# Zero-padded and regrouped small matmuls in a two-block network on one core

## The chip, the core and the metric

The kernel runs on one core of a Trainium2 chip. The metric is the device time of one execution in microseconds, the median of three runs. Five engines work side by side, each through its own queue in program order: TensorE (PE, the matmuls, with its weight loads shown apart as PEld), VectorE (DVE), ScalarE (ACT), GpSimd (POOL) and SyncE (SP, which here issues most of the DMAs).

## The reference

Two networks run one after the other on a sequence of 512 tokens of width 1024, all in float32. The first has two layers. Layer 0 mixes tokens by windowed averages and by an attention of 8 heads (96 query channels, 64 value channels); layer 1 by a neighbourhood attention of 16 heads of 64 channels. Each layer then attends to 256 memory tokens and has an MLP. The second network has two layers of retention (4 heads) and gated linear attention (GLA, 4 heads, keys of 64 channels, values of 128), run forwards and backwards over 512 latent and 256 context tokens, and an MLP. What the change touches is this:

```python
# layer 0 of the first network: attention
p = softmax(s); o = einsum('bhqk,bkhd->bqhd', p, v)          # d = 64
# layer 1: neighbourhood attention
s = einsum('bchd,brckhd->bhcrk', q_row, k_win) * scale + bias # d = 64
# second network: GLA gate, with 16 + 16 gate channels
a = log_sigmoid(d @ up + ub) / 16
# GLA in chunks of 64 tokens, forwards and backwards: within a chunk
#   o += mask(q k^T) v, between chunks o += q S, S <- decay * S + k^T v
```

## The kernel before, in words

Large products are written as three float32r matmuls of high and low halves (`mat3`: hi·hi, hi·lo, lo·hi), from 128x128 weights against 256 or 512 columns. `linear` and `linear_tm` stream the weights for them through SP, ACT (`whi`, L247) and DVE (`wlo`, L248). Attention and GLA use plain float32 matmuls (`mat`, L159) and PE transposes (`tr`, L171). A float32 matmul stands in the trace as two passes (two MATMUL records), a float32r matmul or a transpose as one.

Work is written as Python generators ("streams") that a small planner, `run`, interleaves by an estimated TensorE clock; a `yield 1500` lets other streams go first for about that many ns. A scheduler then fixes each engine's order when the program is built, by its own estimate of times. The result is one fixed order for each engine, in which long runs of float32r matmuls of the projections are mixed with the small matmuls of attention and GLA.

The small matmuls do not use the whole 128x128 array of TensorE. The built program gives each a tile of the array (rows x columns):

- `values` in `mixer0` (L785 to 809): softmax rows are transposed (four `tr` into an `mm` buffer), copied to `PT` by ACT or DVE, and multiplied with the values, 64 output rows of 512 columns: tile 128x64. Heads `hh` 0 and 1 go to different halves of the array's columns. For each of 4 key blocks `j` and 4 pairs of heads there are two such matmuls, 32 in all.
- `unit` in `mixer1` (L940 to 992): scores `pt<-kT,qT` contract over 64 channels: tile 64x128. One tile `qT` holds two heads, one in each half of the rows. There are 64 such matmuls, 32 of 256 and 32 of 192 columns. The products with the values (`po<-PT,v` and `po<-PT,vs`, 128 columns) have tiles 128x64 or 64x64.
- `gla` in `hybrid`: the gate `pt<-dd,gup` contracts over 32 channels (tile 32x128; 8 of 512 columns and 8 of 256). The masked products `pt<-gc,ei` and the state updates `pt<-v,ke` contract over 64 rows (tile 64x128), for two directions or two chunks in different halves of the rows; the forward ones are all written before the backward ones. In the output the products with the states (`po<-S,gc`, tile 128x64, two halves of columns) stand as pairs behind a full matmul `po<-v,gp`:

```python
for i in range(n):
    self.mat(po[:, sl(i)], pr[:, sl(i)], V["g", hd, i], True, False)
    for j in range(2):
        cix = 2 * i + j
        self.mat(po[64 * j:64 * j + 64, sl(i)], c[:, sl(cix, 64)], S[cix], False, True)
```

GLA runs 4 context heads (n = 2 blocks of 128 tokens) and 4 latent heads (n = 4) in layer 0, 4 latent heads with outputs and 4 context heads that only carry the state in layer 1. The matmuls `bank<-ada,sil` (four column quarters of 32, tile 128x32) and `gate_in` (L1263) are of this kind too and stay as they are.

## Time and profile before

| | before |
|---|---|
| median of 3 runs | 3273.99 us (3270.78 to 3279.21) |
| the profiled execution | 3278.94 us |
| its span, first to last instruction | 3277.2 us |
| PE busy | 3195.6 us, 98% |
| PEld busy | 2669.8 us, 81% |
| DVE busy | 1787.2 us, 55% |
| ACT busy | 1204.8 us, 37% |
| POOL busy | 206.9 us, 6% |
| mean granted clock of TensorE | 0.985 of full speed |

Full speed of TensorE's clock is 2.4 GHz, the other level 1.2 GHz. A row of the timeline merges equal instructions that follow each other: its start, the time from the first one's start to the last one's end, and how many passes. A matmul's end is modelled and overlaps the next one's start, so the price of a piece of work is the distance between starts.

### The profile page before, as it was taken

How to read it: one execution, taken by the hardware profiler on the slowest of the kernel's cores; microseconds unless marked ns; L12 is line 12 of the kernel's file. 1: busy time of each engine (PE TensorE's matmuls, PEld its weight loads, DVE VectorE, ACT ScalarE, POOL GpSimd, SP SyncE). 2: the span in 40 equal slices, each digit the busy share in tenths (PEclk: the TensorE clock that was granted, in tenths of full speed). 3: DMA queues.
4: the chain of work that ended last, by engine and by line, in shares of the span. 5: the costliest groups of instructions: out<-in, count | busy, mean ns of one | idle time of the engine just before them, and what ended most of it. 6: DMA issues, size and time to landing. Idle time of an engine off the chain costs nothing.

```text
span 3277.2 us, 45112 instructions
## 1 busy us (share of the span) xinstructions
PE 3195.6 (98%) x17942; PEld 2669.8 (81%) x17942; DVE 1787.2 (55%) x3208; ACT 1204.8 (37%) x2157; POOL 206.9 (6%) x257
## 2 busy tenths in 40 slices
PE   8999999999999999999999999999999989899998
PEld 8856678888987878888988987888888879778887
DVE  6863364445556564445775786333334756774444
ACT  5733242223444432223553534121222534342223
POOL 0100000000112000000021312000000012200000
PEclk9999999999999999999999999999999999899999
DMA  5357743333321223333533221222212423123332
GB/s 155 116 165 240 255 148 99 98 98 102 89 71 53 85 78 97 98 98 91 153 90 88 84 84 58 65 65 65 64 60 60 131 78 97 39 74 98 99 97 71
DMA packets 301858, 323.99 MB, mean 99 GB/s; under 512 B 18832, under 2 KB 270608, under 8 KB 301648
## 3 DMA queue, kind: packets, MB, share of 16 engines
q1 hardware_dynamic: 296656, 315.22, 31.2%
q10 hardware_dynamic: 4992, 5.90, 0.6%
q8 instruction: 141, 2.31, 0.3%
q14 instruction: 69, 0.57, 0.1%
HBM read 310.05 MB, written 2.10 MB: 95 GB/s over the span
## 4 chain that ended last, share of the span: by engine, by line
PE 93%; DVE 3%; ACT 1%; DMA 1%; issue 1%; SPq 0%; ACTq 0%; DVEq 0%
PE mm L159 79%; PE pt L159 6%; PE po L159 4%; PE bank L1032 2%; PE pt L171 1%; PE bank L159 1%; DMA raw<-in_w_mem_kv 1%; PE mm L171 0%; DVE wlo L248 0%; DVE S L1455 0%; DVE sq L366 0%; ACT whi L247 0%; DVE o L1300 0%; DVE ht L1068 0%; DMA ada<-in_ada_w 0%
## 5 line engine op out<-in xcount | busy, mean ns | idle before, releaser
L248 DVE TENSOR_TENSOR wlo<-raw,whi 128x1024 fp32r<-128x1024 f32 (+2 forms) x503 | 595.9, 1186 | 720.3 <-ACT whi L247 690.6
L247 ACT CAST whi<-raw 128x1024 fp32r<-128x1024 f32 (+2 forms) x503 | 505.0, 1006 | 1234.2 <-PE mm L159 1077.5
L159 PE MATMUL mm<-hi,whi 128*128 128x512 f32 (+2 forms) x2768 | 886.5, 357 | 15.3 <-DVE cx L1135 6.1
L159 PE MATMUL mm<-hi,wlo 128*128 128x512 f32 (+2 forms) x2288 | 842.2, 369 | 0.0
L159 PE MATMUL mm<-lo,whi 128*128 128x512 f32 (+2 forms) x1808 | 706.2, 391 | 1.7 <-DVE lo L1073 1.6
L159 PEld LDWEIGHTS mm<-hi,whi 128*128 128x128 f32 (+1 forms) x2768 | 493.8, 190 | 104.5 <-issue 15.2
L159 PEld LDWEIGHTS mm<-hi,wlo 128*128 128x128 f32 (+1 forms) x2288 | 433.4, 190 | 79.7 <-issue 10.0
L159 PE MATMUL mm<-ahi,whi 128*128 128x512 f32 (+1 forms) x1552 | 489.7, 352 | 0.0
L159 PE MATMUL mm<-ahi,wlo 128*128 128x512 f32 (+1 forms) x1296 | 471.8, 366 | 0.0
L159 PEld LDWEIGHTS mm<-lo,whi 128*128 128x128 f32 (+1 forms) x1808 | 340.7, 188 | 77.9 <-issue 7.4
L159 PE MATMUL mm<-alo,whi 128*128 128x512 f32 (+1 forms) x1040 | 399.6, 386 | 0.0
L159 PE MATMUL mm<-whi,hi 128*128 128x256 f32 (+2 forms) x1392 | 368.3, 292 | 17.5 <-ACT v L1207 7.6
L159 PE MATMUL mm<-wlo,hi 128*128 128x256 f32 (+2 forms) x1200 | 346.2, 289 | 2.2 <-DVE wlo L248 2.2
L159 PEld LDWEIGHTS mm<-ahi,whi 128*128 128x128 f32 x1552 | 277.4, 189 | 41.0
L159 PE MATMUL mm<-whi,lo 128*128 128x256 f32 (+2 forms) x1008 | 289.4, 289 | 0.6 <-DVE lo L406 0.6
L159 PEld LDWEIGHTS mm<-whi,hi 128*128 128x128 f32 x1392 | 258.4, 195 | 26.7 <-ACT v L1207 7.8
L159 PEld LDWEIGHTS mm<-ahi,wlo 128*128 128x128 f32 x1296 | 244.4, 189 | 39.4
L159 PEld LDWEIGHTS mm<-wlo,hi 128*128 128x128 f32 x1200 | 234.3, 195 | 9.4 <-issue 5.3
L159 PEld LDWEIGHTS mm<-alo,whi 128*128 128x128 f32 x1040 | 195.5, 188 | 38.1
L159 PEld LDWEIGHTS mm<-whi,lo 128*128 128x128 f32 x1008 | 195.9, 195 | 5.6 <-issue 4.8
L1135 DVE SCALAR_TENSOR_TENSOR x<-mm,mod,x 128x512 f32<-128x512 f32 (+1 forms) x102 | 72.2, 717 | 99.5 <-PE mm L159 99.1
L952 POOL TENSOR_TENSOR bm<-bias,mask 128x192 f32<-128x192 f32 (+1 forms) x64 | 45.5, 735 | 839.5 <-DMA mask<-in_na_mask 643.6
(320 smaller groups left out, 3249.9 us busy)
## 6 DMA issues: line engine op xcount, KB each, us to landing
raw<-in_w_ff SPq DMA_DIRECT2D x128, 512.0 KB, 3.6
raw<-in_w_mlp SPq DMA_DIRECT2D x128, 512.0 KB, 3.6
raw<-in_w_in SPq DMA_DIRECT2D x98, 512.0 KB, 3.8
ada<-in_ada_w SPq DMA_DIRECT2D x192, 256.0 KB, 4.5
raw<-in_w_qkv SPq DMA_DIRECT2D x24, 512.0 KB, 3.7
raw<-in_w_out SPq DMA_DIRECT2D x24, 512.0 KB, 3.4
raw<-in_w_mem_kv SPq DMA_DIRECT2D x32, 256.0 KB, 3.7
raw<-in_w_mem_q SPq DMA_DIRECT2D x16, 512.0 KB, 3.5
```

The lines of the kernel that those rows point to most:

```text
L159: return self.nc.tensor.matmul(out, lhsT=lhsT, rhs=rhs, start=start, stop=stop, **k).ins
L171: self.nc.tensor.transpose(out, in_, self.ident)
L247: nc.scalar.copy(hi[:, v], raw[:, v])
L248: nc.vector.tensor_sub(lo[:, v], raw[:, v], f32(hi[:, v]))
L952: nc.gpsimd.tensor_add(bm[:, sl(hh, 256)][:, :n], o.tab[hp * 2 + hh][:, f0:f0 + n], masks[(0, 1, 1, 2)[b]][:, f0:f0 + n])
L1032: m = nc.tensor.matmul(p[32 * g:32 * g + 32], lhsT=sil[:, k], rhs=w, start=(k == 0), stop=(k == KT - 1), tile_position=(0, 32 * g)).ins
L1135: self.nc.vector.scalar_tensor_tensor(x, p, self.mod[l][:, 16 + 24 * j + m, st:st + 1], x, ALU.mult, ALU.add)
```

## The change

The products of `values` wait until two key blocks are copied and then stand as four matmuls together, the first of them made to wait for the two last copies. The scores of `unit` read a `qT` of 128 rows in which the other head's half is zero (its gain `gg` is zero there), so that each has the full tile 128x128; two ACT copies make two such tiles where one made one. `gup` and `dd` get 128 rows, of which 96 are zero (set by POOL). The two halves of `pt<-gc,ei` and of `pt<-v,ke` are written in turns, and the products with the states stand behind all full matmuls of their output.

```diff
 def values(pr):                                        # mixer0
-            last = None
-            for j in range(5):
-                ts = []
-                for hh in range(2 if j < 4 else 0):
+            ts = []
+            for j in range(4):
+                for hh in range(2):
                     ...
                     t = self.t2(nm="PT")
-                    (nc.vector.tensor_copy if j % 2 else nc.scalar.copy)(t, p)
-                    ts.append(t)
+                    copied = (nc.vector.tensor_copy if hh else nc.scalar.copy)(t, p).ins
+                    ts.append((j, hh, t, copied))
                     self.give("mm")
-                if last:
-                    yield 500
-                    for hh in range(2):
-                        self.mat(po[sl(hh, 64)], vt[pr, j - 1][:, sl(hh, 64)], last[hh], j == 1, j == 4)
-                last = ts
+                if j % 2:
+                    yield 1500
+                    first = None
+                    for j, hh, t, _ in ts:
+                        m = self.mat(po[sl(hh, 64)], vt[pr, j][:, sl(hh, 64)], t, j == 0, j == 3)
+                        first = first or m
+                    self.wait_for(first, ts[-2][3], ts[-1][3])
+                    ts = []
                 yield 0
@@ mixer1
-        ng, gg = self.tiny(2, "ng"), self.tiny(1, "gg")
+        ng, gg = self.tiny(2, "ng"), self.tiny(2, "gg")
         nc.scalar.dma_start(ng, A["na_g"])
-        nc.vector.tensor_scalar(gg, ng[:, 0:1], ng[:, 1:2], 0.125, ALU.mult, ALU.mult)
+        nc.gpsimd.memset(gg, 0.0)
+        for hh in range(2):
+            f = sl(hh, 64)
+            nc.vector.tensor_scalar(gg[f, hh:hh + 1], ng[f, 0:1], ng[f, 1:2], 0.125, ALU.mult, ALU.mult)
...
-                        nc.scalar.activation(t, p, AF.Copy, scale=gg)
-                        o.q.append(t)
+                        o.q.append([self.t2(nm="qT") for _ in range(2)])
+                        for hh, t in enumerate(o.q[-1]):
+                            nc.scalar.activation(t, p, AF.Copy, scale=gg[:, hh:hh + 1])
...
-                rows = slice(64 * hh, 64 * hh + 64)
                 p = self.pt((128, n))
-                self.mat(p, o.q[hp][rows, sl(b)], o.k[hp][rows, k0:k1])
+                self.mat(p, o.q[hp][hh][:, sl(b)], o.k[hp][:, k0:k1])
@@ second network
-        self.gup = self.cst("gup", [32, 4, 128])
+        self.gup = self.cst("gup", [128, 4, 128])
+        nc.gpsimd.memset(self.gup, 0.0)
...
-        nc.scalar.dma_start(self.gup, self.A["gup"][:, l])
+        nc.scalar.dma_start(self.gup[:32], self.A["gup"][:, l])
...
             t = self.t2(nm="dd", w=w)
+            nc.gpsimd.memset(t, 0.0)
             nc.scalar.copy(t[:32], p)
...
-            self.mat(p, self.gup[:, hd], F["d"][:32])
+            self.mat(p, self.gup[:, hd], F["d"])
...
-                for d, s in enumerate((f, r)):
-                    p = self.pt((128, w))
-                    for i in range(n):
+                ps = [self.pt((128, w)) for _ in range(2)]
+                for i in range(n):
+                    for p, s in zip(ps, (f, r)):
                         self.mat(p[:, sl(i)], ei[s, sl(i)], c[s, sl(i)])
+                for d, p in enumerate(ps):
                     nc.vector.copy_predicated(pr, self.gmask[:, d, :w], p)
...
-            for q in range(2):
-                rs = sl(q, 64)
-                p = self.pt((128, n, 128))
-                for i in range(n):
-                    self.mat(p[:, i], ke[rs, sl(i)], V["g", hd, i][rs])
-                    ups[2 * i + q] = p[:, i]
+            ps = [self.pt((128, n, 128)) for _ in range(2)]
+            for i in range(n):
+                for q in range(2):
+                    rs = sl(q, 64)
+                    self.mat(ps[q][:, i], ke[rs, sl(i)], V["g", hd, i][rs])
+                    ups[2 * i + q] = ps[q][:, i]
...
+            k = {"skip_group_check": True}
             for i in range(n):
-                self.mat(po[:, sl(i)], pr[:, sl(i)], V["g", hd, i], True, False)
-                for j in range(2):
-                    cix = 2 * i + j
-                    self.mat(po[64 * j:64 * j + 64, sl(i)], c[:, sl(cix, 64)], S[cix], False, True)
+                self.mat(po[:, sl(i)], pr[:, sl(i)], V["g", hd, i], i == 0, False, **k)
+            for cix in range(nch):
+                i, j = divmod(cix, 2)
+                self.mat(po[64 * j:64 * j + 64, sl(i)], c[:, sl(cix, 64)], S[cix], False, cix == nch - 1, **k)
```

The order of the instructions on PE moves in three places. The rows name the output buffer, the operands and the shape of the output; x2 stands for two equal rows. First, PE in `values` of the first pair of heads, before:

```order
L171 MATMUL mm_2267<-ident,P_1961 128x128
L159 MATMUL po_2245<-PT_2251,v_1511 64x512
L159 MATMUL pt_2330<-hi_1997,hi_1988 128x512
L159 MATMUL pt_2330<-lo_1998,hi_1988 128x512
L159 MATMUL pt_2330<-hi_1997,lo_1989 128x512
L159 MATMUL po_2245<-PT_2258,v_1511 64x512
```

and in the change:

```order
L159 MATMUL pt_2384<-hi_1997,hi_1988 128x512
L159 MATMUL pt_2384<-lo_1998,hi_1988 128x512
L159 MATMUL pt_2384<-hi_1997,lo_1989 128x512
L159 MATMUL po_2245<-PT_2251,v_1511 64x512
L159 MATMUL po_2245<-PT_2258,v_1511 64x512
L159 MATMUL po_2245<-PT_2265,v_1511 64x512
L159 MATMUL po_2245<-PT_2272,v_1511 64x512
L171 MATMUL mm_2328<-ident,P_1877 128x128
```

The four products of two key blocks, which stood apart between scores and transposes, now stand together. Second, PE at the output of GLA head 0 of the latent tokens in layer 0, before:

```order
L159 MATMUL po_15792<-S_15714,gc_15088 64x128 x2
L159 MATMUL po_15792<-v_15248,gp_15566 128x128
L159 MATMUL po_15792<-S_15714,gc_15088 64x128 x2
L159 MATMUL po_15792<-v_15250,gp_15566 128x128
L159 MATMUL po_15792<-S_15715,gc_15088 64x128 x2
L159 MATMUL po_15792<-v_15250,gp_15566 128x128
L159 MATMUL po_15792<-S_15715,gc_15088 64x128 x2
```

and in the change:

```order
L159 MATMUL pt_15754<-v_15269,ke_15711 128x128 x2
L159 MATMUL pt_15754<-v_15271,ke_15711 128x128 x2
L159 MATMUL po_15813<-S_15735,gc_15109 64x128 x4
L159 MATMUL po_15813<-S_15736,gc_15109 64x128 x4
L159 MATMUL mm_15919<-whi_15922,lo_13619 128x256
```

The eight products with the states are one group; the full matmuls `po<-v,gp` have gone ahead of it. Third, PE at the state updates of a latent GLA head of layer 0 (`ke_16897`), before:

```order
L159 MATMUL pt_16930<-v_15412,ke_16897 128x128 x2
L159 MATMUL pt_16930<-v_15414,ke_16897 128x128 x2
L159 MATMUL pt_16935<-v_15412,ke_16897 128x128 x2
L159 MATMUL pt_16935<-v_15414,ke_16897 128x128 x2
L159 MATMUL mm_16987<-wlo_17108,hi_13622 128x256
```

and in the change (the same head is `ke_16918`):

```order
L159 MATMUL pt_16951<-v_15433,ke_16918 128x128 x2
L159 MATMUL pt_16951<-v_15435,ke_16918 128x128 x2
L159 MATMUL po_17063<-v_15433,gp_16756 128x128
L159 MATMUL po_17063<-v_15435,gp_16756 128x128 x2
L159 MATMUL mm_17008<-whi_17128,hi_13636 128x256
L159 MATMUL mm_17008<-wlo_17129,hi_13636 128x256
L159 MATMUL mm_17008<-whi_17128,lo_13637 128x256
L159 MATMUL mm_17008<-whi_17128,hi_13642 128x256
L159 MATMUL mm_17008<-wlo_17129,hi_13642 128x256
L159 MATMUL mm_17008<-whi_17128,lo_13643 128x256
L159 MATMUL mm_17008<-whi_17128,hi_13648 128x256
L159 MATMUL pt_16952<-v_15433,ke_16918 128x128 x2
```

Written in turns, the two halves have come to stand apart in the built order: the second half (`pt_16952`) is behind three full matmuls of the output and seven float32r matmuls.

## Rows read from the trace of the kernel before

**Rows 1.** The page, parts 1 and 4: busy times, and the chain by engine.

```profile
PE 3195.6 (98%) x17942; PEld 2669.8 (81%) x17942; DVE 1787.2 (55%) x3208; ACT 1204.8 (37%) x2157; POOL 206.9 (6%) x257
...
PE 93%; DVE 3%; ACT 1%; DMA 1%; issue 1%; SPq 0%; ACTq 0%; DVEq 0%
```

**Rows 2.** Busy time by stage: us, then busy PE, PEld, DVE, ACT, POOL; clock, DMA share, GB/s.

```profile
150.00:310.00 160.00, 158.72 (x789) 94.00 (x788) 89.06 (x197) 60.40 (x117) 0.31 (x1) 0.99 0.60 195
840.00:1070.00 230.00, 225.11 (x1551) 183.92 (x1550) 138.59 (x393) 103.52 (x260) 41.55 (x58) 0.97 0.22 68
1550.00:1900.00 350.00, 340.03 (x2402) 304.37 (x2400) 244.40 (x441) 164.49 (x291) 59.56 (x62) 0.98 0.36 102
2520.00:2850.00 330.00, 306.37 (x2001) 267.58 (x2000) 216.10 (x392) 141.57 (x246) 44.27 (x46) 0.93 0.30 86
```

**Rows 3.** Timeline of PE, two value products together: start us, us, instruction (rows x columns).

```profile
176.16 0.39 PE L159 MATMUL mm<-lo,whi 128*128 128x512 f32 x1
176.38 0.39 PE L159 MATMUL mm<-hi,wlo 128*128 128x512 f32 x1
176.70 1.08 PE L159 MATMUL po<-PT,v 128*64 128x512 f32 x4
177.71 0.50 PE L159 MATMUL pt<-hi,hi 96*128 96x512 f32 x1
```

**Rows 4.** Timeline of PE, one value product alone.

```profile
158.40 1.07 PE L159 MATMUL po<-PT,v 128*64 128x512 f32 x2
```

**Rows 5.** Timeline of PE: sixteen passes of the modulation, four to each column quarter.

```profile
254.74 1.92 PE L1032 MATMUL bank<-ada,sil 128*32 128x512 f32 x16
```

**Rows 6.** Timeline of PE, scores: alone (256, 192 columns) and a pair (192).

```profile
852.49 0.28 PE L159 MATMUL mm<-wlo,hi 128*128 128x256 f32 x1
852.70 0.70 PE L159 MATMUL pt<-kT,qT 64*128 64x256 f32 x2
853.32 0.39 PE L159 MATMUL mm<-whi,lo 128*128 128x256 f32 x1
...
873.47 0.59 PE L159 MATMUL pt<-kT,qT 64*128 64x192 f32 x2
...
1039.61 0.59 PE L159 MATMUL pt<-kT,qT 64*128 64x192 f32 x4
```

**Rows 7.** Timeline of PE, full-array float32 matmuls of the memory attention.

```profile
358.75 1.03 PE L159 MATMUL pt<-mk,q 128*128 128x256 f32 x4
359.61 1.88 PE L159 MATMUL po<-PT,mv 128*128 128x512 f32 x4
361.33 1.03 PE L159 MATMUL pt<-mk,q 128*128 128x256 f32 x4
```

**Rows 8.** Timeline of PE, the gate's matmul: 256 and 512 columns.

```profile
1645.09 0.69 PE L159 MATMUL pt<-dd,gup 32*128 32x256 f32 x2
...
1694.33 1.12 PE L159 MATMUL pt<-dd,gup 32*128 32x512 f32 x2
```

**Rows 9.** Timeline of PE: two pairs (neighbourhood values) and one pair (GLA states).

```profile
909.41 0.66 PE L159 MATMUL po<-PT,vs 128*64 128x128 f32 x8
...
1606.25 0.44 PE L159 MATMUL po<-S,gc 128*64 128x128 f32 x4
```

**Rows 10.** Timeline of PE: halves of four and four passes, one of eight, two of eight.

```profile
1592.69 0.72 PE L159 MATMUL pt<-gc,ei 64*128 64x128 f32 x8
...
1739.89 1.16 PE L159 MATMUL pt<-gc,ei 64*128 64x128 f32 x8
...
1880.89 1.71 PE L159 MATMUL pt<-v,ke 64*128 64x128 f32 x16
```

**Rows 11.** Groups by line: copies to PT and to qT (busy us, mean ns, idle before).

```profile
L798 DVE COPY PT<-mm 128x512 f32<-128x512 f32 x16 | 11.0, 686 | 10.0 <-PE mm L171 8.8 <-PE po L159 1.2
...
L933 ACT ACTIVATE qT<-pt,gg 128x512 f32<-128x512 f32 x8 | 5.3, 685 | 4.7 <-PE mm L159 2.6 <-PE pt L171 2.2
```

**Rows 12.** Longest wait of PE from 2520 to 2850 us: total, times, longest.

```profile
PE mm L159 <- ACT v L1207: 7.6, 1, 7.6
```

More of the change, by code (lines that the diff above doesn't have):

```diff
@@ L930, in transposes @@
                         self.tr(p[:, sl(i)], o.tm[nm, i // 2][:, sl(i % 2, 256)][:, sl(j)])
-                    t = self.t2(nm=nm + "T")
                     if nm == "q":
-                        nc.scalar.activation(t, p, AF.Copy, scale=gg)
-                        o.q.append(t)
+                        o.q.append([self.t2(nm="qT") for _ in range(2)])
+                        for hh, t in enumerate(o.q[-1]):
+                            nc.scalar.activation(t, p, AF.Copy, scale=gg[:, hh:hh + 1])
                     else:
+                        t = self.t2(nm="kT")
                         nc.vector.tensor_copy(t, p)
```

## The prediction

> **What bounds the kernel now.** TensorE does. On the page PE is busy for 98% of the span and 93% of the chain that ended last is PE [rows 1]; DVE has 55% and ACT 37%. In the stages that the change touches (150 to 310 us: attention of layer 0; 840 to 1070: neighbourhood attention; 1550 to 1900 and 2520 to 2850: the GLA layers) PE stands idle for 1.3, 4.9, 10.0 and 23.6 us, while DVE has at most 244 of 350 us of work [rows 2]. So what counts is how much time of PE's queue each small matmul takes. The order of instructions on PE is fixed when the kernel is built; outside these stages the two programs hardly differ.
>
> The next view is the timeline of PE, read by starts. A float32r matmul of 512 columns starts 0.22 us after the one before (176.16, 176.38). The value products on half of the columns start 0.32 after it, at 176.70: about 0.09 us more. They hold PE until 177.71 [rows 3]. Around the score it is the same: the float32r matmul of 256 columns, elsewhere 0.12 us, is followed after 0.21 us, and the next one starts 0.62 us after the score [rows 6]. So a stretch on a part of the array costs about 0.09 us at its entry, some more inside and at its exit. Its **price**, the distance from the start before it to the start behind it less the step that the matmul before needs anyway, is 177.71 - 176.38 - 0.23 = 1.10 us in rows 3 and 853.32 - 852.49 - 0.12 = 0.71 in rows 6. Both are the row's own length plus 0.02 (1.08, 0.70), and I use that sum for the other stretches.
>
> Full-array float32 passes have no such step: four of 256 columns take 359.61 - 358.75 = 0.86, that is 0.43 for a matmul of two passes; four of 512 take 1.72, 0.86 for a matmul [rows 7].
>
> **The change, part by part.** How often each kind of stretch stands in PE's queue I counted in the two fixed orders.
>
> Value products of layer 0. Of 32 matmuls 8 pairs stand together and 16 matmuls alone: 24 stretches. A pair costs 1.10 [rows 3], one alone 1.09 [rows 4]: a pair on two halves of the columns runs side by side, and the lone one pays for both. Three of the lone ones touch a stretch of the modulation and share its step, so 26.1 us in all. Now there are 8 stretches of four. Sixteen passes, four to each column quarter, cost 1.94 [rows 5]; eight passes on two halves are also four to each part, so I take 1.94 and get 15.5. If a second pair cost as much as a first (2.20) it would be 17.6. Term: -10.6, bound -8.5. The new wait for both last copies stands behind 2 us or more of other PE work in all 8 places, and a copy takes 0.69 us [rows 11]; that cover hides it, and if DVE were late the transposes behind it would wait too.
>
> Scores. 28 of 64 stand alone, 22 of 256 and 6 of 192 columns: 22 x 0.72 + 6 x 0.61 = 19.5 [rows 6]. With all rows they cost 0.43 for 256 [rows 7]; a full float32 pass of 192 columns is in no row, it lies between 0.22 (128 columns, half of 0.43) and 0.43, and by columns at 0.33: 22 x 0.43 + 6 x 0.33 = 11.4. That is -8.1. The other 36 stand in pairs or beside value products. A pair of 192 costs 0.61 now (0.59 + 0.02, [rows 6]) and 0.66 padded, so each of 18 pairs loses 0.05, 0.9 in all. Term: -7.2; bounds -4 (192 columns as dear as 256, and another 2 us of steps at the value products that now stand alone) and -9. On ACT come 8 copies of 0.69 us [rows 11], 5.5 us beside 103.5 of 230 [rows 2]; TensorE waits for them only at a group's start.
>
> The row of the pair speaks against padding, and so does a rule of the Trainium skill (TensorEngine Tiling (Array Packing), When to Use Tiling): with a contraction of 64 or less, tile the rows two ways, for up to twice the speed. By it the scores would stay in halves and be brought together instead. By the rows, 32 pairs at the price of a pair would be at best level with 64 padded ones; padding wins because the built order parts 28 of them.
>
> Gate. 8 matmuls of 512 columns at 1.14 and 8 of 256 at 0.71 are 14.8, less 0.7 for four that touch another small stretch: 14.1 [rows 8]. Full: 8 x 0.86 + 8 x 0.43 = 10.3 [rows 7]. Term: -3.8. The memsets on POOL (12% busy there, [rows 2]) are short and early.
>
> States in the GLA output. 40 pairs at 0.46 are 18.4; two pairs cost 0.68, so a further pair 0.22 [rows 9]. Now 8 groups of four pairs (0.46 + 0.66 = 1.12) and 4 of two: 11.7. Term: -6.7.
>
> Masked products. Halves in sequence already overlap in part: four and four passes cost 0.74, one half of eight 1.18, and two of eight 1.73, not 2.36 [rows 10]. The context heads stand as before. Of 8 latent heads 4 stood together and 4 apart: 4 x 1.73 + 4 x 2.36 = 16.4. Now 3 stand in turns (0.74 + 2 x 0.22 = 1.18), one nearly so (1.4), 1 together, 3 apart: 13.8. Term: -2.6.
>
> That overlap is against a rule of the Trainium skill (TensorE: Matmul & The Clock Gate, Part 3, The mechanism): matmuls start and end strictly in program order. By it two halves of eight in sequence would cost 2.06 us (sixteen steps of 0.11 and the 0.30 that 1.18 has beyond eight), not 1.73, and the term would be some 1 us larger.
>
> State updates. Of 8 latent heads 3 stood together (1.73), none does now: the scheduler parts them, as the third order above shows. Term: 3 x 0.63 = +1.9. Written in turns and not standing in turns, this part does not do what it says.
>
> Sum: -10.6 - 7.2 - 3.8 - 6.7 - 2.6 + 1.9 = **-29.0 us** of PE's queue. Not all of it shortens the span: where PE waits for others (23.6 of 330 us in the last stage, [rows 2], the longest of them 7.6 us for ACT [rows 12]) a faster PE waits longer. I take 3 us back, about a quarter of what the GLA terms bring. The profiled execution took 3278.94 us (span 3277.2); less 26 it is 3252.9. The median of the runs is 4.95 us below the profiled one, so **3248 us**.
>
> **Rivals.** *Half of it turns into waits.* The GLA layers hold long chains between PE, DVE and ACT; all of their net 11.2 us and part of the scores' could come back as idle time. Against: the first stage and the scores have hardly any idle time [rows 2]. Time: 3274 - 29 + 13 = 3258.
>
> *Groups on halves do not overlap when they are long.* Then eight value passes cost 0.24 + 8 x 0.43 = 3.7 us (8 x 3.7 = 29.6, +3.5 instead of -10.6) and four state pairs 0.24 + 16 x 0.11 = 2.0, two 1.1 (8 x 2.0 + 4 x 1.1 = 20.4, +2.0 instead of -6.7): 3274 - 29 + 14 + 9 = 3268, no change that can be told. Against: the sixteen passes at 1.94 [rows 5].
>
> *Slower: the joint wait for the copies.* PE's queue is in order, so if at the 8 groups of value products the later copy is late, all float32r work behind it stands. It decides from 3.6 us a group on (29 / 8). At the length of the longest wait in rows 12, 7.6 us, it would be +61: 3274 - 29 + 61 = 3306. For: DVE and ACT also do the softmax of that stage. Against: DVE has 89 us of work in 160 [rows 2] and PE waits little there now.
>
> **How the numbers follow.** Forecast (3236 to 3256, the bounds of the terms and up to 8 us of waits) 0.74; half into waits 0.15; no overlap 0.06; slower 0.05. The likeliest gives 3248. Both ends outside the forecast are widened for small shifts of order elsewhere: 3233 to 3262. A measurement can tell about 0.3%, 10 us, so faster means below 3264: 0.74, 0.14 of the second and 0.01 of the third, 0.89; the same 0.07; slower 0.04.
>
> **What would show it.** The timeline should have `po<-PT,v x8` near 1.92 us, `po<-S,gc x16` near 1.10, scores as `128*128` rows with 0.22 us between their starts for 256 columns, and no steps around scores and gates. PE's busy time should fall by about 29 us, its idle time (81 us) rise by a few. The forecast is wrong if the x8 and x16 rows are much longer, if PE's idle time from 150 to 310 us grows by more than 5 us, or if the padded scores cost more than 0.43.

## The result and the profile after

| | before | after |
|---|---|---|
| median | 3272.39 us (3268.49 to 3279.21, 4 runs) | 3230.85 us (3229.87 to 3239.15, 4 runs) |
| after / before | | 0.9876, 95% interval 0.9853 to 0.9900 |
| profiled execution, its span | 3278.94 us, 3277.2 us | 3230.51 us, 3228.7 us |

The change takes 41.5 us off where 26 were forecast; 3230.85 lies 2 us below the lower end of the widened range (3233). The page of the changed kernel, parts 1 and 4, against [rows 1]:

```profile
PE 3146.0 (97%) x17942; PEld 2664.6 (83%) x17942; DVE 1779.2 (55%) x3209; ACT 1210.6 (37%) x2165; POOL 212.3 (7%) x263
...
PE 92%; DVE 5%; ACT 1%; DMA 1%; issue 1%; POOL 0%; DVEq 0%; SPq 0%; ACTq 0%; POOLq 0%
```

TensorE still sets the end. The profiled execution of before was a long one; a second profile of the same kernel (the run before_again, span 3269.6) lies nearer to the median, and the stages are compared with that. They are cut at the same instructions of every program: attention of layer 0; the stage of the scores, from the first score to the last memory attention of that layer; the first GLA layer; the stretch up to the next; the second GLA layer. The columns are those of [rows 2]. The kernel before, once more:

```profile
111.08:322.58 211.50, 208.42 (x1098) 134.83 (x1097) 130.78 (x332) 98.26 (x212) 6.37 (x16) 1.00 0.56 183
...
843.97:1154.91 310.94, 306.05 (x1924) 249.08 (x1924) 178.19 (x482) 142.22 (x341) 41.56 (x58) 0.98 0.23 70
...
1560.91:1906.85 345.94, 334.93 (x2368) 298.66 (x2367) 244.20 (x451) 160.94 (x287) 59.52 (x62) 0.98 0.34 100
1906.85:2542.04 635.19, 624.41 (x3625) 551.22 (x3623) 280.67 (x446) 192.10 (x328) 28.72 (x30) 1.00 0.21 66
2542.04:2828.04 286.00, 266.53 (x1797) 234.28 (x1797) 186.83 (x330) 117.34 (x198) 37.57 (x34) 0.95 0.31 90
```

and the changed kernel:

```profile
110.10:309.02 198.92, 194.59 (x1098) 134.31 (x1097) 130.30 (x333) 98.35 (x213) 6.84 (x18) 1.00 0.60 196
...
830.49:1129.12 298.63, 291.81 (x1924) 249.79 (x1923) 179.57 (x482) 145.94 (x347) 40.58 (x58) 1.00 0.24 73
...
1535.04:1866.23 331.19, 321.67 (x2348) 292.92 (x2346) 238.50 (x448) 160.96 (x287) 60.45 (x63) 0.99 0.36 102
1866.23:2505.02 638.79, 629.17 (x3647) 556.06 (x3644) 283.68 (x450) 192.57 (x329) 29.12 (x32) 0.99 0.22 67
2505.02:2786.79 281.77, 260.09 (x1798) 235.00 (x1797) 182.30 (x325) 117.39 (x198) 39.19 (x34) 0.94 0.33 92
```

The first two stages are 12.6 and 12.3 us shorter. The last three belong together (in the changed kernel 20 or so float32r matmuls stand behind the cut between them instead of ahead of it): 1267.1 us become 1251.8, 15.4 less. The other stages differ by 0.7 us in all. The terms of the forecast were 10.6, 7.2 and 11.2. Two things are to be seen beside that. Over all nine stages, which are nearly the whole run, PE's busy time fell by 43.5 us (3188.8 to 3145.3), while its idle time (length less busy) rose by 2.5 (67.1 to 69.6): by 1.3 in the first stage shown and 1.9 in the second, while in the last three it went from 41.3 to 40.8. And the clock column of the scores' stage went from 0.98 to 1.00: before has 10.2 us at half clock (0.50 of full speed) there by the clock records of its trace, the changed kernel none.

The new forms cost what was taken for them; the old ones had cost more. The timeline of PE in the changed kernel, a value group and scores, against [rows 3 to 7]:

```profile
161.18 1.94 PE L159 MATMUL po<-PT,v 128*64 128x512 f32 x8
...
834.57 0.28 PE L159 MATMUL mm<-wlo,hi 128*128 128x256 f32 x1
834.69 0.60 PE L159 MATMUL pt<-kT,qT 128*128 128x256 f32 x2
834.93 0.47 PE L159 MATMUL mm<-whi,lo 128*128 128x256 f32 x1
835.24 0.28 PE L159 MATMUL mm<-whi,hi 128*128 128x256 f32 x1
```

Eight passes of a value group last 1.94 (taken: 1.94). A padded score starts 0.12 after the matmul ahead of it, without the step of 0.09; from 834.57 to 835.24 are 0.67, less two float32r steps of 0.12 the score costs 0.43, the value taken. This span reaches to the second start behind the score. The price of a lone score before, 0.71, was read to the first start behind it. The kernel before goes on behind the score of [rows 6] with

```profile
853.55 0.28 PE L159 MATMUL mm<-whi,hi 128*128 128x256 f32 x1
853.66 0.29 PE L159 MATMUL mm<-wlo,hi 128*128 128x256 f32 x1
```

and behind the value products of [rows 3] with

```profile
178.05 0.39 PE L159 MATMUL pt<-lo,hi 96*128 96x512 f32 x1
```

The matmul behind the score, at 853.32, holds PE for 0.23 us until the next start, where such a matmul elsewhere holds it for 0.12; the one behind the value products, at 177.71, for 0.34 instead of 0.23. So a stretch on a part of the array has a step of 0.11 at its end too, and the step falls on the matmul behind it. Over the same span as in the change a lone score costs 853.55 - 852.49 - 2 x 0.12 = 0.82, and padding it brings 0.39 and not 0.28.

In the first GLA layer, against [rows 8 to 10]:

```profile
1576.58 0.66 PE L159 MATMUL po<-S,gc 128*64 128x128 f32 x8
...
1728.15 1.09 PE L159 MATMUL po<-S,gc 128*64 128x128 f32 x16
...
1819.33 1.02 PE L159 MATMUL pt<-dd,gup 128*128 128x512 f32 x2
...
1832.45 1.16 PE L159 MATMUL pt<-gc,ei 64*128 64x128 f32 x16
...
1844.51 1.16 PE L159 MATMUL pt<-v,ke 64*128 64x128 f32 x8
1846.75 1.16 PE L159 MATMUL pt<-v,ke 64*128 64x128 f32 x8
```

Four state pairs take 1.09 (taken: 1.12 with the steps), and a masked product in turns takes 1.16 for sixteen passes, as long as one half of eight alone. The two halves of a state update stand apart at 1.16 each, as the built order had shown. The full matmuls of the output, `po<-v,gp`, got cheaper with the state pairs. Between two pairs, before (the first pair is in [rows 9]), and together, in the change:

```profile
1606.62 0.49 PE L159 MATMUL po<-v,gp 128*128 128x128 f32 x2
1607.04 0.44 PE L159 MATMUL po<-S,gc 128*64 128x128 f32 x4
...
1732.27 1.06 PE L159 MATMUL po<-v,gp 128*128 128x128 f32 x8
1733.08 0.36 PE L159 MATMUL mm<-whi,hi 128*128 128x256 f32 x1
```

Between two pairs one of them holds PE for 0.42 us; four together hold it for 0.81, which is 0.20 each.

The lengths of the groups (1.94, 1.09 and 1.16) tell against strict sequence (the Trainium skill, TensorE: Matmul & The Clock Gate, Part 3, The mechanism): passes on different parts of the array overlap here even when each part gets four or eight of them.

### The profile page after: what moved, and what is told of

It reads as the page before. It is cut to its first block, busy times and chain, and to the rows that moved or that the text cites. A ratio compares the mean times of both kernels' runs of the same rounds, so it can differ in the third digit from the quotient of the medians.

```text
span 3228.7 us, 45138 instructions
## 1 busy us (share of the span) xinstructions
PE 3146.0 (97%) x17942; PEld 2664.6 (83%) x17942; DVE 1779.2 (55%) x3209; ACT 1210.6 (37%) x2165; POOL 212.3 (7%) x263
## 4 chain that ended last, share of the span: by engine, by line
PE 92%; DVE 5%; ACT 1%; DMA 1%; issue 1%; POOL 0%; DVEq 0%; SPq 0%; ACTq 0%; POOLq 0%
PE mm L159 78%; PE pt L159 5%; PE po L159 3%; PE bank L1037 1%; PE pt L171 1%; PE bank L159 1%; DVE wlo L248 1%; DVE S L1463 1%; DMA raw<-in_w_mem_kv 1%; DVE ht L1073 1%; PE mm L171 0%; DVE o L1307 0%; DMA x<-in_x 0%; ACT whi L247 0%; DVE sq L366 0%
## 5 line engine op out<-in xcount | busy, mean ns | idle before, releaser
L159 PEld LDWEIGHTS mm<-ahi,wlo 128*128 128x128 f32 x1296 | 244.4, 189 | 39.4
L1567 DVE TENSOR_TENSOR relu<-relu 128x512 f32<-128x512 f32 (+1 forms) x98 | 56.7, 593 | 76.7 <-ACT ahi L1566 76.7
```

The source lines that it names most:

```text
L159: return self.nc.tensor.matmul(out, lhsT=lhsT, rhs=rhs, start=start, stop=stop, **k).ins
L1567: nc.vector.tensor_mul(t, t, t)
```

## The experiments

Intervals are 95% intervals of the ratio to the kernel before, which ran beside them on the same chip in each comparison (its medians 3269.5 to 3274.2).

**The parts alone.** Four kernels: the kernel before; only the part in `values`; only the part in `mixer1` (the two `qT` and `gg`); only the four parts of the GLA layers. Each edit is that part of the diff shown above and nothing else, so the core of each is:

```diff
+                if j % 2:                                                    # values_only
...
+                    for j, hh, t, _ in ts:
+                        m = self.mat(po[sl(hh, 64)], vt[pr, j][:, sl(hh, 64)], t, j == 0, j == 3)
...
+                self.mat(p, o.q[hp][hh][:, sl(b)], o.k[hp][:, k0:k1])        # scores_only
...
+            for cix in range(nch):                                           # gla_only
+                i, j = divmod(cix, 2)
+                self.mat(po[64 * j:64 * j + 64, sl(i)], c[:, sl(cix, 64)], S[cix], False, cix == nch - 1, **k)
```

> The kernel before once more, for its profile. Theory 'idle time': the stretches at half the granted clock at 304, 915 and 1058 us (17 us of them from 150 to 1070 us) and the idle time of the profile before belong to the kernel; this profile shows them again, within a few us. Rival 'one execution': they belong to the one profiled execution, which at 3278.94 us was 6.5 us above the median; this profile has a span near 3270 us and hardly any half-clock time from 150 to 1070 us.

> Of the change only the grouping of the value products in layer 0. Theory 'steps': what is saved is the price of the small stretches alone, 24 stretches of 1.10 us against 8 of 1.94 us: -11 us. Theory 'steps and idle time': also what PE waits for between the stretches falls (3.8 us of the stage's 15.3 us in the profile after): -15 us.

> Of the change only the padded scores. Theory 'steps': -7 us by the forecast's term, with no half-clock time counted. Theory 'steps and idle time': the stage from 840 to 1070 us keeps the full clock, as in the profile after, where 13.6 us at half clock are gone: -14 us, and no half-clock stretch in that stage.

> Of the change only the parts in the gated linear attention: gate, turns, grouped state products. Theory 'steps': the sum of the forecast's terms, -11 us (in the profile after the small stretches cost 8.5 us less). Theory 'steps and idle time': -16 to -20 us, most of it in the first of the two layers, where the profile after has 8.8 us less beside the stretches. Rival 'waits come back': -5 us or less.

| run | median | ratio and interval | against before |
|---|---|---|---|
| before_again | 3270.66 | 0.9994 (0.9983 to 1.0005) | none |
| values_only | 3260.50 | 0.9960 (0.9947 to 0.9972) | -13.7 us |
| scores_only | 3264.30 | 0.9970 (0.9958 to 0.9982) | -9.9 us |
| gla_only | 3253.29 | 0.9933 (0.9919 to 0.9948) | -20.9 us |

The parts sum to -44.5, the whole gives -41.5: within the noise they add up. By these times only the GLA part is clear of its term. Its interval stands for 17 to 27 us, against a term of 11.2; those of the value products (9 to 17) and of the scores (6 to 14) hold their terms of 10.6 and 7.2, and before_again, which is the kernel before, itself ran 3.6 us below the median that the last column is taken against.

The profiles show more. In before_again the half clock near 914 and 1054 us is back (10.2 us of it), the one at 304 is not, and the span is 3269.6, so neither theory holds whole. The stage of `values` is 198.62 us in values_only, 12.9 less than before; PE's idle time there rose by 0.9, so the theory in which it falls is out. In gla_only the last three stages lose 15.6 us, 14.3 of them in the first layer; the second theory has the place and nearly the size, but the gain is busy time (15.4) and not idle time. In scores_only the stage of the scores is as long as in the whole change, 298.62 (12.3 less than before), at full clock, as the second theory has it, but the second GLA layer, whose code is that of before, came out 7 us longer:

```profile
2528.93:2821.87 292.94, 268.95 (x1803) 237.00 (x1803) 189.01 (x332) 118.60 (x199) 38.03 (x34) 0.93 0.31 89
```

PE's idle time there is 24.0 us (19.5 before) and its clock 0.93 (0.95). So a stage without any edit can move by 7 us; half clock there lasts 39.9 us instead of 30.2, which can be 4.8 of them.

**The whole without the scores' part.** The edit takes `mixer1` back:

```diff
-                self.mat(p, o.q[hp][hh][:, sl(b)], o.k[hp][:, k0:k1])
+                self.mat(p, o.q[hp][rows, sl(b)], o.k[hp][rows, k0:k1])
```

> The whole change, but with the scores of neighbourhood attention as before: on 64 rows, not padded. Theory A (each part brings what its own stretches on PE cost, and no more): the padding's 7.2 us come back, 3231 + 7 = 3238 us, and the clock of that stage is as in the changed kernel. Theory B (the padding also takes away the stretches of half clock between 840 and 1070 us, 5 us in the comparison of the whole change): 3231 + 12 = 3243 us, and the profile shows half clock there again, as in the four profiles so far with unpadded scores and in neither of the two with padded ones.

Measured 3243.13 us, 0.9921 (0.9908 to 0.9933): 12 us above the changed kernel's 3231, the time of theory B. Its mechanism hardly showed: there is half clock for 3.4 us only, at 1040. The stage is 308.11 us long, 9.5 more than with padding, of which half clock can be 1.7; the rest of the 12 lies in stages without the edit, 2.3 of it in the first 106 us.

**The GLA parts alone, and the clock.** The edits are the last hunk of the diff (states), the two written in turns (turns) and `gup` with `dd` (gate).

```diff
-                for j in range(2):                                           # states_only
-                    cix = 2 * i + j
+            for cix in range(nch):
+                i, j = divmod(cix, 2)
...
+                    for p, s in zip(ps, (f, r)):                             # turns_only
...
+            self.mat(p, self.gup[:, hd], F["d"])                             # gate_only
```

> Before, with the two state products of a chunk pair written next to each other in the GLA output, and nothing else. Theory A (steps alone): -6.7, some 3267.5 us against 3274. Theory B (this part also takes the waits of 8 us out of the first GLA layer, since it brings the output of a head forward): 3259 us, with PE's idle time between 1550 and 1900 us down by 8 us.

> Before, with the halves of the masked products and of the state updates written in turns, and nothing else. Theory A (steps alone): -2.6 + 1.9 = -0.7, 3273.5 us. Theory B (the order in turns lets the copies of the masks run while PE works, and takes the waits of 8 us out of the first GLA layer): 3265 us, with PE's idle time between 1550 and 1900 us down by 8 us.

> Before, with the gate's matmul padded to all rows, and nothing else. Theory A (steps alone): -3.8, 3270.4 us. Theory B (the gate is the head of the chain of a GLA head, and a gate that ends earlier takes the waits out of the first GLA layer): 3262 us, with PE's idle time between 1550 and 1900 us down by 8 us.

| run | median | ratio and interval | last three stages | PE busy in them | PE idle |
|---|---|---|---|---|---|
| before_again | 3270.66 | 0.9994 (0.9983 to 1.0005) | 1267.1 | 1225.9 | 41.3 |
| states_only | 3254.43 | 0.9958 (0.9944 to 0.9972) | 1253.4 | 1214.0 | 39.4 |
| turns_only | 3272.86 | 1.0008 (0.9997 to 1.0020) | 1268.2 | 1225.6 | 42.6 |
| gate_only | 3272.01 | 1.0010 (1.0000 to 1.0019) | 1268.4 | 1225.3 | 43.0 |
| gla_only | 3253.29 | 0.9933 (0.9919 to 0.9948) | 1251.5 | 1210.5 | 41.0 |

The state products carry the layers: 13.7 us alone, twice their term. That is nearer to theory B in time, but not for its reason, since idle time fell by 2 us only and busy time by 12. Turns give nothing, as forecast. The gate alone gives nothing either, though its term was 3.8: PE's busy time in the two GLA layers fell by 3.3 us, but in the stretch between them it grew by 2.8, with the clock at 0.99 instead of 1.00, and the end of the program grew by 3.5. Half clock lasts 56 us in the three stages of gate_only and 47 in before_again; that can be 4.4 us, more than the term.

The profiles of turns_only and gate_only showed something else. In the stage of the scores, where their code is that of before, they are 306.7 us long and have full clock throughout. So the half clock there does not belong to unpadded scores, and theory B of the run without the scores' part fell in its general form. Two more profiles were to tell chance from program.

> The kernel with only the gate padded once more, whose profile showed no half clock in the stage of the scores though the scores are as before. Theory A (a property of the program): none again, the stage 306.7 us long. Theory B (comes and goes with the execution): as in the profiles of the kernel before, 5 to 7 us lost there, the stage 311 to 313 us long.

> The changed kernel once more. Theory A (no half clock in the stage of the scores is a property of the padded program): 3231 us, the stage again 298.6 us long, full clock in it. Theory B (half clock comes and goes with the execution): half clock may stand there in this one, and the stage is 302 to 305 us long.

Gate_again: 306.68 us, no half clock, like its first profile. After_again: 3230.87 us, 0.9883 (0.9865 to 0.9901), stage 298.60, no half clock, like its first. Both profiles of before have it, from about 915 and from about 914 us, for 13.7 and 10.2 us in the stage. In these three programs, with two profiles of each, it came or stayed away with the program and not with the execution. Here is the same place in two programs, cut into three stretches (us, busy PE, PEld, DVE, ACT, POOL, clock). The kernel before, once more:

```profile
905.00:913.70 8.70, 7.73 (x71) 6.00 (x69) 2.58 (x6) 3.90 (x9) 2.28 (x4) 1.00 0.18 59
913.70:920.50 6.80, 6.80 (x32) 5.60 (x32) 3.82 (x19) 2.69 (x11) 1.41 (x2) 0.50 0.00 0
920.50:930.00 9.50, 9.50 (x70) 7.74 (x68) 6.40 (x20) 4.56 (x11) 1.90 (x2) 1.00 0.19 57
```

and gate_again, with the same instructions up to there but for one memset of `gup` on POOL at its start:

```profile
903.70:912.40 8.70, 7.73 (x71) 6.00 (x70) 2.54 (x7) 3.82 (x9) 2.28 (x4) 1.00 0.19 61
912.40:919.20 6.80, 6.80 (x48) 5.35 (x48) 4.62 (x26) 4.27 (x15) 1.42 (x2) 1.00 0.00 0
919.20:928.70 9.50, 9.50 (x73) 8.03 (x73) 7.64 (x19) 5.88 (x14) 3.05 (x4) 1.00 0.36 112
```

The two first rows agree to the hundredth of a us on PE, 71 matmuls in 7.73 us. Then one program gets a clock of 0.50 (1.2 GHz) and does 32 matmuls in 6.8 us, the other keeps full clock and does 48. The work just before is thus not what tells them apart. Nor is the memset: gla_only has it too, and 10.2 us of half clock. The instructions of turns_only and of states_only on PE, DVE, ACT and POOL are those of before up to this place, in the same order, and their stages begin at 842.64 and 842.70 us; the first has full clock, the second 13.7 us of half clock. What tells the programs apart, no run here settles.

**Pairing instead of padding.** The scores stay on halves of the rows, and a full transpose into each of the two buffers holds both back until both buffers are free, so that all stand in pairs:

```diff
-                self.mat(p, o.q[hp][hh][:, sl(b)], o.k[hp][:, k0:k1])
+            pp = [self.pt((128, n)) for _ in range(2)]
...
+            with self.tc.issue_after(self.touch(pp[0], q)), self.tc.issue_after(self.touch(pp[1], q)):
+                for hh in range(2):
...
+                    self.mat(pp[hh], q[rows, sl(b)], kk[rows, k0:k1])
```

> The changed kernel without the padding of the scores, but with a full transpose into each of the two PSUM buffers of a unit ahead of its scores, and both half scores held back behind them, so that all 32 pairs stand together. Theory A (steps): against the padded form 24 pairs of 256 columns gain 0.13, 8 of 192 gain 0.05, 64 transposes of 0.11 cost 7.0: +3.5, 3234.5 us; the pairs by themselves, without the transposes, would then be level with the padding or better. Theory B (half clock comes back in the stage as soon as the scores are on half of the rows): +8.5, 3239.5 us.

Measured 3241.74 us, 0.9913 (0.9900 to 0.9925). The stage:

```profile
831.60:1140.93 309.33, 300.25 (x1985) 245.78 (x1985) 178.13 (x482) 141.09 (x341) 40.51 (x58) 0.99 0.23 71
```

and one pair in its timeline, between a transpose and float32r matmuls:

```profile
835.53 0.27 PE L175 MATMUL pt<-ident,qT 128*128 128x128 f32 x1
835.73 0.70 PE L159 MATMUL pt<-kT,qT 64*128 64x256 f32 x4
836.36 0.39 PE L159 MATMUL mm<-whi,hi 128*128 128x256 f32 x1
836.58 0.28 PE L159 MATMUL mm<-wlo,hi 128*128 128x256 f32 x1
```

Read to the first start behind it, a pair of 256 costs 0.73, as theory A has it; read to the second, 836.58 - 835.53 - 0.11 - 0.12 = 0.82, against two padded ones at 0.86. The 3.5 us that theory A took as the gain of the pairs are then some 0.5 (an estimate: 24 x 0.04, less 8 x 0.06 for the pairs of 192). The stage is 10.7 us longer than the padded one. The 64 transposes are 7.0 of that (0.11 each), half clock at 899 can be 1.7, and the rest, 2.0, is about the growth of PE's idle time (9.1 against 6.8). Theory A is too low. The time of theory B is within the interval (3237 to 3245), but its cause is not there: half clock lasts 3.4 us. For the rule that speaks for two row tiles (the Trainium skill, TensorEngine Tiling (Array Packing), When to Use Tiling) this is half a confirmation: the pair itself is cheaper, as its row says, but here it had to be brought together, and that cost more than it saved. Without the transposes and the half clock PE's work is level with the padded form (291.5 and 291.8 us, an estimate), and the stage 2 us longer by its waits.

**One part out of the whole.** The edits undo the last hunk, and `gup` with `dd`:

```diff
-            for cix in range(nch):                                           # no_states
+                for j in range(2):
...
-            self.mat(p, self.gup[:, hd], F["d"])                             # no_gate
+            self.mat(p, self.gup[:, hd], F["d"][:32])
```

> The whole change without the state products written next to each other in the GLA output. Theory A (the term by steps): 3231 + 6.7 = 3237.7 us. Theory B (as this part did alone, where it gave 13 us, by shorter steps and by waits and half clock that moved elsewhere): 3231 + 13 = 3244 us. What tells them apart inside: PE's busy time from the first GLA layer to the end of the second, and the half clock there.

> The whole change without the padding of the gate. Theory A (the term by steps): 3231 + 3.8 = 3234.8 us. Theory B (as this part did alone, where PE's busy time in the GLA layers fell by 3.3 us and the run got no shorter): 3231 us.

No_states: 3247.76 us, 0.9931 (0.9919 to 0.9944), 17 above the changed kernel. Half clock in the stage of the scores is back (10.2 us of it; the stage takes 302.87 us, 4.2 more), padded though the scores are. The three last stages:

```profile
1540.12:1886.68 346.56, 333.66 (x2368) 299.95 (x2366) 243.17 (x451) 160.75 (x287) 59.44 (x63) 0.98 0.36 100
1886.68:2521.86 635.18, 624.34 (x3626) 551.24 (x3625) 283.27 (x446) 191.87 (x328) 27.21 (x32) 1.00 0.21 66
2521.86:2804.60 282.74, 261.92 (x1798) 231.64 (x1797) 182.35 (x330) 117.54 (x198) 38.46 (x34) 0.96 0.33 91
```

They are 1264.5 us, 12.7 more than in the changed kernel: 9.0 of PE's busy time (1219.9 against 1210.9) and 3.7 of idle time. Half clock does not explain them: in the three stages it lasts 44 us here and 49 in the changed kernel. Theory B holds for this part, in either company. No_gate: 3236.46 us, 0.9896 (0.9881 to 0.9910). Its last three stages are 5.2 us longer than those of the changed kernel (busy time 5.5), over the term of 3.8; half clock lasts 49 us in both. So the gate's gain is there in this company, and did not show alone.

**Can the same be had for the masked products and the updates?** First both halves of each were brought together, by transposes as above:

```diff
+            with self.tc.issue_after(self.touch(ps[0][:, 0], b)), self.tc.issue_after(self.touch(ps[1][:, 0], b)):
+                for i in range(n):
+                    for q in range(2):
...
+                        self.mat(ps[q][:, i], ke[rs, sl(i)], V["g", hd, i][rs])
```

> The changed kernel, with one full transpose of 128 columns put into each of the two PSUM buffers of a masked product and of a state update, and all half matmuls of the two held back on PE behind both, so that in the built order they stand next to each other in turns (16 groups of state updates, 12 of masked products, all whole). Theory A (halves in turns cost what a row of eight next to eight, or four next to four, shows: 1.18 and 0.74): state updates 8 x (2.36 - 1.18) + 5 x (1.46 - 0.74) = -13.0, masked products 3 x 1.18 + 0.55 = -4.1, 56 transposes of 0.11 = +6.2, together -11: 3220 us. Theory B (PE now waits for the later of two buffers, which is why they stood apart, and the gain is given back as idle time in the GLA layers): 3231 us or more.

Measured 3238.09 us, 0.9899 (0.9886 to 0.9913): slower than the changed kernel by 7 us. The halves stand as meant, sixteen passes in the time of eight:

```profile
1722.75 1.16 PE L159 MATMUL pt<-v,ke 64*128 64x128 f32 x16
```

PE's waits in the two GLA layers of this kernel, the first layer's two longest, then those of the second for DVE's states `S` (total us, times, longest):

```profile
PE mm L159 <- DVE cx L1144: 5.1, 2, 3.0
PE po L159 <- DVE S L1469: 3.3, 1, 3.3
...
PE pt L175 <- DVE S L1469: 6.3, 1, 6.3
PE po L159 <- DVE S L1469: 5.0, 2, 3.3
```

and the waits for `S` in the changed kernel, first layer and second:

```profile
PE pt L159 <- DVE S L1463: 2.5, 1, 2.5
...
PE pt L159 <- DVE S L1463: 4.8, 1, 4.8
...
PE po L159 <- DVE S L1463: 0.4, 1, 0.4
```

In the three stages PE's busy time fell by 6.6 us and its idle time rose by 14.7. The states, which DVE computes from the updates, now hold PE up for 3.3 us in the first layer and 11.3 in the second, instead of 2.5 and 5.2. That is 6.9 of the 14.7; of the rest, 3.4 is a longer wait for `cx` in the first layer (5.1 us, 1.7 in the changed kernel). Theory B holds. That it is the wait for the later buffer which delays the updates was not measured by itself.

Then the updates were padded. The next kernel shares one pair of zero-padded tiles among all heads, without keeping the heads apart: a head's keys can be overwritten by the next one's before they are read, so that part of the computation is changed. To make room for the tiles it also has 11 instead of 14 buffers for tiles of 256 columns (`NT1`).

```diff
-NT1 = 14
+NT1 = 11
...
+            ke = self.kez[0]
+            for q in range(2):
+                nc.scalar.copy(ke[q][sl(q, 64), :w], p[sl(q, 64)])
...
+                    self.mat(p[:, i], ke[q][:, sl(i)], V["g", hd, i])
```

> The changed kernel with the state updates padded as well: the keys of the two halves are copied into two tiles whose other half is zero for the whole program, and the eight half matmuls of a head become eight full ones in two groups, wherever they stand. Theory A (steps; a full float32 matmul of 128 columns is 0.215): latent heads 8 x (2 x 0.86 - 2.36) = -5.1, context heads 5 x (0.86 - 1.46) + 3 x (0.86 - 0.74) = -2.6, together -7.7: 3223 us. Theory B (the only pair of padded tiles makes a head's copies wait for the updates of the head before, and the gain is given back as idle time): 3231 to 3238 us, with PE's idle time in the GLA layers up.

Measured 3231.50 us, 0.9877 (0.9860 to 0.9894), the time of the changed kernel: busy time in the three stages down by 6.5 us, idle time up by 8.1. These are theory B's numbers, but its cause is not in the trace: no copy into the shared tiles waits for the updates of another head (in the first layer ACT fills them for two heads at 1707.58 and 1713.55, before the first updates from them at 1718.17). The wait that grew most is that for DVE's `gb` in the second layer, 8.0 us instead of 3.8. Whether the fewer buffers, the shared tiles or the order of the heads made it grow was not tested. The last kernel gives each head two tiles of its own.

```diff
-            ke = self.t2(nm="ke", w=w)
-            nc.scalar.copy(ke, p)
+            ke = [self.t2(nm="ke", w=w) for _ in range(2)]
+            for q in range(2):
+                nc.gpsimd.memset(ke[q][sl(1 - q, 64)], 0.0)
+                nc.scalar.copy(ke[q][sl(q, 64)], p[sl(q, 64)])
...
-                    self.mat(ps[q][:, i], ke[rs, sl(i)], V["g", hd, i][rs])
+                    self.mat(p[:, i], ke[q][:, sl(i)], V["g", hd, i])
```

> The changed kernel with the state updates padded, each head with two tiles of keys of its own (the other half zeroed by POOL per head), so no head waits for another's tiles. Theory A (the idle time of the run before came from the shared tiles; PE's time is what counts): 3231 - 7.7 = 3223 us. Theory B (in the GLA layers the heads' chain over ACT, DVE and PE sets the end of the last head, and PE time saved on the updates comes back as idle time whatever holds the keys): 3229 to 3232 us, PE's busy time in the two layers down by 6 to 8 us and its idle time up by as much.

Measured 3224.18 us (3223.37 to 3227.81, 4 runs), 0.9856 (0.9840 to 0.9873): theory A in its time, and below both kernels in every run. The last three stages:

```profile
1535.76:1869.82 334.06, 322.48 (x2372) 297.28 (x2370) 240.56 (x450) 165.87 (x296) 65.25 (x79) 0.98 0.37 103
1869.82:2506.30 636.48, 625.52 (x3623) 552.16 (x3620) 282.85 (x448) 191.36 (x328) 30.54 (x36) 0.99 0.22 66
2506.30:2781.62 275.32, 254.25 (x1799) 232.87 (x1797) 182.74 (x325) 121.52 (x206) 42.19 (x46) 0.96 0.34 94
```

The first two together are 0.6 us longer than in the changed kernel: 2.8 us less PE work, 3.4 more idle time. The second GLA layer is 6.5 us shorter, 5.8 of it busy time, with its clock at 0.96 instead of 0.94: half clock lasts 23 us there instead of 32, which can be 4.5 of the 6.5. So the time is theory A's, but how much of it the padding brought is not shown. In the first layer and the stretch behind it, PE time saved came back as idle time, as theory B has it.

## Why the prediction was wrong

The sign, the place and the mechanism were right; the size was not. The step that failed is the price of a small stretch, "the distance from the start before it to the start behind it": the stretch has a step of about 0.11 us at its end too, which falls on the matmul behind it and is seen only at the second start behind. The text names an exit, but its price ends ahead of it. So the old forms cost more than the sum had them at, and more is saved. Point by point, against the second profile of before:

- **"Sum: ... = -29.0 us of PE's queue"**: PE's busy time fell by 43.5 us, 14.5 more. Of these 4.3 are the clock of the scores' stage, which the sum put at nothing: at full clock, with the code unchanged, the stage is 306.7 us long (gate_again), at the clock of before 310.9. The other 10.2 are 3.2 in the stage of the value products, 2.8 in that of the scores, 3.7 in the GLA layers and 0.5 elsewhere. The step that the price left out, 0.11 us each, is gone at 16 stretches of value products, 28 lone scores, 28 stretches of states and 16 gates, by the prediction's own counts: an estimate of 9.7 us.
- **Value products**, -10.6: the stage lost 12.6 (13.8 of busy time, 1.3 more idle time), with the groups at the 1.94 taken. 16 steps are 1.8 us (an estimate). Another 1.9 are the modulation's matmuls, which the edit does not touch: they stand in 22 stretches instead of 23 in this stage, and their busy time is 26.8 us instead of 28.7. The cover for the joint wait held: the slower rival's 7.6 us a group are nowhere.
- **Scores**, -7.2: compared at full clock, the stage goes from 306.7 us (gate_again) to 298.6, which is -8.1. But that is busy time down by 10.0, past the bound of -9, and idle time up by 1.9, which the sum had in another term. 28 steps are 3.1 us (an estimate).
- **States**, -6.7: the term that was furthest out. Summed from start to start, the pairs and the full matmuls between them hold PE for 33.0 us in before_again and 22.8 in states_only, 33.0 in no_states and 22.6 in the changed kernel: 10.3 less by this edit in either company, 6.1 of them at the full matmuls. A pair between two full matmuls cost 1607.04 - 1606.25 - 0.20 = 0.59, not 0.46. The three stages lost 13.7 us by this part alone, and 12.7 when it was taken out; the difference to the 10.3 was not traced to rows.
- **Gate, masked products, updates**, -3.8, -2.6 and +1.9: alone, gate and turns gave no gain; taken out of the whole the gate costs 5.2. With 16 steps its term would be some -5.5 (an estimate). Whether that reaches the span depends on the rest. POOL's share beside the gate, 12% in the text, is 17% and 13% by [rows 2]; nothing hangs on it.
- **"I take 3 us back"** was right in size and wrong in place: PE's idle time rose by 2.5 us, but in the stages of the value products and the scores, where the text saw hardly any, and not in the GLA layers (41.3 us before, 40.8 after). The first rival (half turns into waits) fell with it. It was not wrong in kind: in joined_halves and in padded_updates 6.6 and 6.5 us of PE's work were saved in the GLA layers and 14.7 and 8.1 of idle time came.

So of the 41.0 us between the two profiles 29.0 were the sum, 4.3 the clock in the stage of the scores and 10.2 what the prices left out and order elsewhere, less 2.5 of waits. The 4.3 are luck as far as is known: half clock stands in that stage of three other kernels with padded scores (no_states, no_gate, joined_halves), and two with unpadded ones have none (turns_only, gate_only). Why one program gets half clock at a place and another does not stays open. Single surpluses of 2 to 4 us are smaller than the 7 us by which a stage without any edit moved in scores_only; the step at the end of a stretch does not rest on them but on the rows.

The rival of groups that do not overlap fell by the rows of 1.94 and 1.09. Of the signs that the text named, PE's idle time from 150 to 310 us up by more than 5 did not appear, and PE's idle time over the whole did rise by a few. Its busy time, which should have fallen by about 29 us, fell by 43.5: that sign was missed, and it is the one that points at the prices.

## What to carry to other kernels

Price a small matmul by the distance between the starts around it, up to the start from which the matmuls behind run at their usual step, and count how often it stands alone in the built order. Read one start too short, the prices here left out some 10 of 39 us. Where a scheduler parts the halves, padding with zeros is robust, since a padded matmul needs no partner beside it (0.43 for a score alone between float32r matmuls); holding halves back so that they meet adds a wait, and in chains over several engines that can cost more than it saves. Before a difference between two profiles is put down to an edit, compare the granted clock and PE's idle time of each stage, also of the stages without an edit.

## What the runs showed of the hardware

A stretch of matmuls on half of the array cost a step on either side: about 0.09 us ahead of it and 0.11 us behind, where the next full matmul held PE for 0.23 us instead of 0.12 (256 columns) or 0.34 instead of 0.23 (512 columns).

The same 71 matmuls in the same 7.73 us were followed by half clock in one program and full clock in another, and each did the same again in a second execution. In the profiles of all kernels but paired_scores, the stage of the scores is 298.6 to 298.7 us long with padding at full clock, up to 302.9 with padding and stretches of half clock (no_states), 306.7 without padding at full clock, and up to 312.6 without padding and with such stretches (the first profile of before).
